# A decoder layer on one Trainium2 core: low parts of u finished in HBM by an adding DMA, and two more pairs by seven products

## The chip, the cores and the metric

The kernel runs on one core of one Trainium2 chip. The metric is the device time of one execution in microseconds. A core has five engines that each work through their own instructions in order: TensorE (PE, the matrix products), VectorE (DVE), ScalarE (ACT), GpSimd (POOL) and SyncE (SP). In this kernel SP and POOL mostly issue DMAs. Each engine waits on semaphores that the others, or landing DMAs, raise.

## The reference, cut to what matters

One decoder layer on 256 tokens of width 2048: a norm, an input projection, two attention groups, an output projection, and then the MLP, which is where the change lies:

```python
h = _rmsnorm(x, norm_mlp_pre[layer])
u = jnp.square(jax.nn.relu(h @ w_up[layer]))      # (256, 2048) @ (2048, 8192)
x = x + _rmsnorm(u @ w_down[layer], norm_mlp_post[layer])   # (256, 8192) @ (8192, 2048)
```

All arrays are float32.

## The kernel before

**Three products for one.** TensorE takes operands rounded to a shorter float format (`fp32r`). Each float32 operand `x` is therefore kept as a high part `hi`, which ACT makes by a rounding copy (line 306, or 310 with a gain), and a low part `lo = x - hi`, which DVE makes by a subtraction (line 307 or 311). A product then is three matmuls into one PSUM bank: hi·hi, hi·lo, lo·hi (`three`, line 1016).

**Weights.** `Weights` streams the weights of the whole program in one order. A tile is 128 rows by 1024 columns (512 KB); SP loads it into one of five buffers `raw`, ACT and DVE split it into one of eight pairs `hi`, `lo`. The load and the split of a tile are written at the same place of the program, six tiles ahead of the tile's use (`emit`, line 193). Because SP only issues loads, it runs further ahead than that, by as much as the five buffers allow.

**Pairs by seven products.** Two neighbouring weight tiles form a pair. Taken directly, a pair costs 2 tiles x 4 output banks x 3 = 24 matmuls of 512 columns. Taken by seven products (`seven_products`, line 1021; a Strassen-like scheme on 2x2 blocks) it costs 7 x 3 = 21, but needs sums of weights and of the left operand: three additions on DVE for the weights, four split tiles instead of two, and for the down projection `down_sums` and `down_split` for u. The two weight tiles of a pair are loaded by POOL as one DMA of 1 MB into `ab` and `ab2` (up projection) or `ab_down` and `c` (down projection).

**Up projection.** Eight blocks j = 0..7 of 1024 columns (line 1051). Blocks 2 to 6 each take tiles k8 to k11, then pair w0, k12, w1, k13, w2, k14, w3, k15. At the end of a block DVE adds the parts of the seven products to the four accumulators (lines 1043 and 1109), and the block's results are evacuated while the next block runs: `up_evac` (line 933) makes `r` = relu on ACT (line 937), has PE transpose it (`rt`, line 300), and ACT squares the transposed piece into `uT[g]` (line 949). Block j yields the two groups g = 2j and 2j+1 of u, 128 x 1024 each (4 k-tiles x 256 tokens), which stay in SBUF. `r` has two buffers.

**Down projection.** Two halves c = 0, 1 of 1024 output columns. Each runs over 64 k-tiles, four to a group g (`DOWN_STEPS`, line 120); `DOWN_SEVEN` (line 117) says which pairs go by seven products. `split_u` (line 951) prepares `uhi` and `ulo` of the next group, each with two buffers. In the first half ACT makes `uhi` and DVE makes `ulo`; `keep_u` (line 965) then has SP store `ulo` to HBM (`ukeep`), and in the second half POOL loads it back (line 960), so that DVE need not make it again. The split sums of pairs that are in both lists are kept in HBM in the same way (`SHARED`, `keep_s`, `down_back`).

**What sets the order.** The program is written in one thread of Python that follows the matmuls; `Flow` (line 128) holds a clock of estimated matmul time, and chains such as `up_evac` are generators that yield delays in microseconds. A chain's next piece is written into the engines' instruction streams when that clock has passed its time. Each engine then executes its stream strictly in that order.

Of the kernel before, what the change touches and what calls it, by code (L numbers as in the profile page):

```python
# [18 lines left out]
F32 = mybir.dt.float32  # L19
F32R = mybir.dt.float32r  # L20
I32 = mybir.dt.int32
BF16 = mybir.dt.bfloat16
AF = mybir.ActivationFunctionType
OP = mybir.AluOpType
PSUM = bass.MemoryType.PSUM

P = 128
# [18 lines left out]
CW = 1024  # L46
# [55 lines left out]
def up_steps(first, *groups):  # L102
    steps = [("k", k) for k in first]
    for i, ks in enumerate(groups):
# [9 lines left out]
N_SEVEN = [sum(w == "w" for w, _ in steps) for steps in UP_STEPS]  # L114


DOWN_SEVEN = ((7, 11, 13, 17, 19, 23, 25, 29), range(3, 28, 2))
SHARED = [k for k in DOWN_SEVEN[0] if k in DOWN_SEVEN[1]]
GT = FF // 512
DOWN_STEPS = [[s for kp in range(2 * GT)  # L120
               for s in ([("w", kp)] if kp in ws else [("k", 2 * kp), ("k", 2 * kp + 1)])] for ws in DOWN_SEVEN]

# [141 lines left out]
def layer(nc, tc, io):  # L264
    flow = Flow()
# [8 lines left out]
    dram = tc.alloc_tile_pool(name="dram", bufs=1, space=bass.MemoryType.DRAM)  # L274
# [3 lines left out]
    def bank(i, name):  # L278
        return ps.tile([P, 512], F32, tag=f"bank{i}", bufs=1, name=name)
# [19 lines left out]
    def transpose(out, a):  # L299
        nc.tensor.transpose(out, a, ident)  # L300
        flow.spend(TR)

    def split(hi, lo, src, g=None):
        if g is not None:
            return split_gain(hi, lo, src, g)
        nc.scalar.activation(hi, src, AF.Copy)  # L306
        nc.vector.tensor_tensor(out=lo, in0=src, in1=hi.bitcast(F32), op=OP.subtract)  # L307
# [6 lines left out]
    def tok(t, k, b):  # L314
        return t[:, k, b * P:(b + 1) * P]
# [28 lines left out]
    late = {}  # L344
# [85 lines left out]
    def seven_down(c, kp):  # L430
        def load():

            n = DOWN_SEVEN[c].index(kp)
            raw = dpl["ab"]
# [246 lines left out]
    for half in range(2):  # L681
        qkv = {}
        for nms in (("qk", "v") if not half else "qkv"):
            accs = [acc for _, _, acc in proj(xT, [ch_a[half, nms]], f"{nms}{half}",
                                              bank_of=at_bank if (half, nms) == (0, "v") else None)]
            for i, nm in enumerate(nms):
                t = pa.tile([P, NB, 512], F32, tag=nm, name=f"{nm}_{half}")
# [215 lines left out]
    for ns in ((0, 1), (2,), (3,)):  # L903
# [4 lines left out]
        for c, b, acc in proj(mixT, [ch_o[n] for n in ns], f"o{ns[0]}", order, heads_done):  # L908
            n = ns[c]
            if not late:  # L910
# [8 lines left out]
                                  in_=io["norm_attn_post"].partition_broadcast(P).rearrange("p o d -> p (o d)"))  # L919
# [8 lines left out]
    hT = late["hT"]  # L928


    uT = {}

    def up_evac(j, b, i, acc, order):

        yield UP_STEP * order
        r = late["up"].tile([P, 512], F32, tag="r", bufs=2, name=f"r{j}_{b}")
        nc.scalar.activation(r, acc, AF.Relu, scale=rstd2[b])
        yield D_UP if j > 1 else 2 * D_UP
        t = bank(i, f"rt{j}_{b}")
        for k in range(4):  # L940
            transpose(t[:, k * P:(k + 1) * P], r[:, k * P:(k + 1) * P])
        if j not in uT:
            if j in (0, 1, 10, 11, 12, 13):
                t2 = late["u01" if j < 2 else "ab2" if j < 12 else "ab"][:, j % 2 * CW:(j % 2 + 1) * CW]
            else:
                tag = {"tag": "T", "bufs": 2} if j > 13 else {}
                t2 = late["up"].tile([P, CW], F32, name=f"uT{j}", **tag)
            uT[j] = t2.rearrange("p (k s) -> p k s", k=4)
        nc.scalar.activation(uT[j][:, :, b * P:(b + 1) * P], t.rearrange("p (k s) -> p k s", k=4), AF.Square)

    def split_u(c, g):
        if (c, g) == (0, 0):
            uh, ul = [wp.tile([P, CW], F32R, tag=w, bufs=W_BUFS, name=f"u{w}0").rearrange("p (k s) -> p k s", k=4)
                      for w in ("hi", "lo")]
        else:
            uh, ul = [dpl["dp"].tile([P, 4, S], F32R, tag=f"u{w}", bufs=2, name=f"u{w}{c}_{g}") for w in ("hi", "lo")]
        u, h, l = [x.rearrange("p k s -> p (k s)") for x in (uT[g], uh, ul)]
        if c and g:
            nc.scalar.activation(h, u, AF.Copy)
            nc.gpsimd.dma_start(out=l.bitcast(F32), in_=ukeep[g])  # L960
        else:
            split(h, l, u)
        return uh, ul

    def keep_u(g):
        ukeep[g] = dram.tile([P, CW], F32, name=f"ukeep{g}")
        nc.sync.dma_start(out=ukeep[g], in_=us[0, g][1].rearrange("p k s -> p (k s)").bitcast(F32))

    def keep_s(kp):
        st, skeep[kp] = skeep[kp], dram.tile([P, CW], F32, name=f"skeep{kp}")  # L970
# [50 lines left out]
    def seven_products(ts, left, accs, m, first, last, m_first=False):  # L1021

        (a11, a12, a22), (s3, s1, s2, s4) = left
        prods = ((a11, 0, 0, 1), (a12, 1, 0, (0, 0)), (s4, 1, 1, (0, 1)), (s2, 2, 0, 6), (a22, 2, 1, (1, 0)),
                 (s3, 3, 1, 7), (s1, 3, 0, 5))
        if m_first:
            prods = sorted(prods, key=lambda x: not isinstance(x[3], int))
        for p, (a, i, half, to) in enumerate(prods):
            w = weights.get(ts[i])
            in_m = isinstance(to, int)  # L1030
            three(m[to] if in_m else accs[to], a, [w[x][:, half * 512:half * 512 + 512] for x in range(2)],
                  in_m and first, in_m and last)
            if all(x[1] != i for x in prods[p + 1:]):
                weights.free(ts[i])
            flow.pump()

    def close(c, m):

        tt = nc.vector.tensor_tensor
        nc.scalar.activation(c[0], m[1], AF.Copy)  # L1040
        for out, x, y, op in ((1, m[6], c[0], OP.subtract), (2, m[7], c[1], OP.subtract),
                              (3, m[5], c[2], OP.subtract), (1, m[5], c[1], OP.add)):
            tt(out=c[out], in0=x, in1=y, op=op)
        return dict(zip(PARTS, c))

    def closing():
        return [late["c"][:, i * 512:(i + 1) * 512] for i in range(4)]
# [3 lines left out]
    for j in range(FF // CW):  # L1051
# [9 lines left out]
        for t, b in order:  # L1061
            what, k, tiles = steps[t]
# [9 lines left out]
            if (j, t, b) == (FF // CW - 1, 4, 0):  # L1072
                weights.limit -= 1
                u_next = split_u(0, 0)
# [39 lines left out]
    up = late["up"]  # L1114
# [5 lines left out]
    def down_mm(c, u, k, b, n, w, first, last):  # L1120
        three(y[b][2 * c + n], [tok(u[x], k % 4, b) for x in range(2)], [t[:, 0, n * 512:n * 512 + 512] for t in w],
              first, last)

    def spare(i, n):

        return uT[i + n // 2].rearrange("p k s -> p (k s)")[:, (n % 2) * 512:(n % 2) * 512 + 512]
# [66 lines left out]
    late["st"] = up.tile([P, ST], F32, tag="st", bufs=1, name="st_down")  # L1193
    dpl["ab"] = dp.tile([P, 2 * CW], F32, name="ab_down")

    us, ukeep = {(0, 0): u_next}, {}
    for c in range(2):

        for i, (b, n) in enumerate(PARTS):
            y[b][2 * c + n] = bank(4 * c + i, f"y{b}{2 * c + n}")  # L1200
        accs = {(b, n): y[b][2 * c + n] for b, n in PARTS}
        ws = DOWN_SEVEN[c]
        for t, (what, k, tiles) in enumerate(wide_d[c]):
            g = (2 * k if what == "w" else k) // 4
            u = us[c, g]
            if g >= GT - 2 and c:
                break
            if what == "k":
                w = weights.get(tiles[0])
                for b, n in PARTS:  # L1210
                    down_mm(c, u, k, b, n, w, t == 0, t == len(wide_d[c]) - 1)
                    flow.pump()
                weights.free(tiles[0])
            else:
                if k == ws[0]:
                    if not c:
                        flow.finish(*u_last)
                    else:
                        flow.finish(h_evac)
                    m = {i: bank(4 * (1 - c) + o, f"md{i}_{c}") for o, i in enumerate((1, 6, 7, 5))}  # L1220
                blocks = [[tok(u[x], 2 * (k % 2) + kk, bb) for x in range(2)] for kk, bb in ((0, 0), (1, 0), (1, 1))]
                seven_products(tiles, (blocks, left.pop((c, k))), accs, m, k == ws[0], k == ws[-1])
                if k == ws[-1]:
                    more = close([spare(10, i) for i in range(4)] if c else closing(), m)
                if not c and k in SHARED:
                    keep_s(k)
            nxt = (c, g + 1) if g < GT - 1 else (1, 0)
            if nxt not in us:
                if not c and g > 1:
                    keep_u(g - 1)  # L1230
                us[nxt] = split_u(*nxt)
            if (c, what, k) == (0, "k", 3):
                weights.limit += 1
            if (c, what, k) == (0, "k", 36):
                g_half = [late["up"].tile([P, 512], F32, tag="r", bufs=2, name=f"g_half{n}") for n in range(2)]
                for n in range(2):
                    load_gain(n, g_half[n])
            if (c, what, k) == (1, "k", 40):
                flow.start(x_back())
                for n in (2, 3):  # L1240
                    load_gain(n, spare(4, n))
        if not c:
            keep_u(GT - 1)
            h_evac = flow.start(half_evac(more, g_half))

    tail = {k: tiles[0] for what, k, tiles in wide_d[1] if k >= 4 * (GT - 2) and what == "k"}
    for g in (GT - 2, GT - 1):
        for b, n in PARTS:
            for kk in range(4):
                k = 4 * g + kk  # L1250
# [58 lines left out]
```

## Time and profile before

| | |
|---|---|
| median of 3 runs | 1047.59 us (1047.38 to 1048.04) |
| profiled execution, its span | 1045.7 us |
| PE busy | 1035.7 us, 99% of the span |
| DVE busy | 838.7 us, 80% |
| ACT busy | 630.4 us, 60% |
| up projection, blocks 0 to 7 | about 354 to 701 us of the span |
| down projection, first half | about 702 to 861 us |
| down projection, second half | about 861 to 1039 us |

The span is that of one profiled execution, from its first to its last instruction; the median is of runs without the profiler and 1.9 us longer. A row of the time line gives start, duration, engine, line, operation, out<-in with shapes, and in brackets the idle time of the engine just before, with what ended it. "SPq" is SP's instruction queue.

### The profile page before, as it was taken

What the parts mean: (1) busy time and instruction counts of PE and PEld (TensorE: products, weight loads), DVE (VectorE), ACT (ScalarE), POOL (GpSimd) and SP (SyncE); (2) the same over time, 40 slices, a digit from 0 to 9 for tenths busy, and PEclk for the clock granted to TensorE, in tenths of its full rate; (3) what the DMA queues carried; (4) which work ended last, traced back from release to release, by engine and by line L of the source; (5) the groups of instructions that cost most, each with busy time, mean ns of one, the idle gap of its engine ahead of it and who ended that gap; (6) DMA issues with size and microseconds to landing.
All of it is one profiled execution on the core that took longest, in us unless ns stands there. A gap on an engine that the chain in (4) does not pass through costs nothing.

```text
span 1045.7 us, 13378 instructions
## 1 busy us (share of the span) xinstructions
PE 1035.7 (99%) x4837; PEld 863.2 (83%) x4837; DVE 838.7 (80%) x1122; ACT 630.4 (60%) x848; POOL 51.5 (5%) x83
## 2 busy tenths in 40 slices
PE   9999999999999999999999999999999999999996
PEld 6888889888888888888888888888888888888885
DVE  6676536567557669999999999897899978999995
ACT  6674436565545566665765667666567564766661
POOL 0000000000000000000000000000000000111100
PEclk9999999999999999999999999999999999999998
DMA  9975547454447295646657356378778767698952
GB/s 303 370 229 148 140 129 241 146 162 153 150 156 236 92 360 188 216 147 207 202 185 246 121 201 207 113 253 325 274 276 303 265 232 261 238 332 323 356 204 83
DMA packets 79938, 229.33 MB, mean 219 GB/s; under 512 B 6912, under 2 KB 11520, under 8 KB 79488
## 3 DMA queue, kind: packets, MB, share of 16 engines
q1 hardware_dynamic: 64576, 171.47, 48.9%
q0 software_dynamic: 14864, 56.63, 15.2%
q8 instruction: 38, 0.62, 0.3%
q10 hardware_dynamic: 432, 0.37, 0.1%
q14 instruction: 28, 0.23, 0.1%
HBM read 212.72 MB, written 15.73 MB: 218 GB/s over the span
## 4 chain that ended last, share of the span: by engine, by line
PE 97%; DVE 1%; issue 1%; ACT 0%; POOL 0%; DVEq 0%; POOLq 0%; ACTq 0%
PE y L296 25%; PE acc_u L296 24%; PE acc_o L296 8%; PE m L296 7%; PE md L296 5%; PE acc_qk L296 4%; PE acc_v L296 4%; PE acc_ckv L296 2%; PE acc_ukv L296 2%; PE acc_q L296 2%; PE acc_cq L296 2%; PE acc_k L296 2%; PE acc_uq L296 2%; PE rt L300 1%; PE sc_b L296 1%
## 5 line engine op out<-in xcount | busy, mean ns | idle before, releaser
L307 DVE TENSOR_TENSOR lo<-raw,hi 128x1024 fp32r<-128x1024 f32 (+3 forms) x213 | 241.5, 1152 | 89.8 <-ACT hi L306 89.1
L306 ACT ACTIVATE hi<-raw 128x1024 fp32r<-128x1024 f32 (+3 forms) x213 | 209.9, 999 | 73.6 <-PE y L296 16.1
L296 PE MATMUL y<-hi,uhi 128*128 128x512 f32 x370 | 144.4, 390 | 0.0
L296 PE MATMUL y<-hi,ulo 128*128 128x512 f32 x370 | 144.1, 389 | 0.0
L296 PE MATMUL y<-lo,uhi 128*128 128x512 f32 x370 | 144.0, 389 | 0.0
L296 PE MATMUL acc_u<-hi,hT_hi 128*128 128x512 f32 x356 | 141.7, 398 | 0.0
L296 PE MATMUL acc_u<-hi,hT_lo 128*128 128x512 f32 x356 | 139.2, 391 | 0.4 <-DVE hT_lo L307 0.4
L296 PE MATMUL acc_u<-lo,hT_hi 128*128 128x512 f32 x356 | 138.9, 390 | 0.0
L311 DVE SCALAR_TENSOR_TENSOR lo<-raw,gcol,hi 128x1024 fp32r<-128x1024 f32 x74 | 92.5, 1279 | 9.5 <-ACT hi L310 9.5
L310 ACT ACTIVATE hi<-raw,gcol 128x1024 fp32r<-128x1024 f32 x74 | 83.7, 1148 | 25.0 <-DMA raw<-in_w_up 11.7
L296 PEld LDWEIGHTS y<-hi,ulo 128*128 128x128 f32 x370 | 69.5, 188 | 14.4
L296 PEld LDWEIGHTS y<-lo,uhi 128*128 128x128 f32 x370 | 69.5, 188 | 14.3
L296 PEld LDWEIGHTS y<-hi,uhi 128*128 128x128 f32 x370 | 69.5, 188 | 14.2
L296 PEld LDWEIGHTS acc_u<-hi,hT_lo 128*128 128x128 f32 x356 | 66.8, 188 | 14.9 <-DVE hT_lo L307 0.8
L296 PEld LDWEIGHTS acc_u<-lo,hT_hi 128*128 128x128 f32 x356 | 67.0, 188 | 12.8
L296 PEld LDWEIGHTS acc_u<-hi,hT_hi 128*128 128x128 f32 x356 | 67.0, 188 | 12.8
L306 ACT ACTIVATE hi<-u 128x1024 fp32r<-128x1024 f32 (+1 forms) x38 | 37.4, 990 | 49.2 <-DVE u L366 35.4
L307 DVE TENSOR_TENSOR lo<-st_down,hi 128x1024 fp32r<-128x1024 f32 x42 | 50.4, 1220 | 3.0 <-ACT hi L306 2.8
L296 PE MATMUL acc_o<-hi,mixT_hi 128*128 128x512 f32 x128 | 51.8, 405 | 0.0
L306 ACT ACTIVATE hi<-st_down 128x1024 fp32r<-128x1024 f32 x42 | 43.9, 1052 | 12.6 <-PE y L296 9.5
L296 PE MATMUL acc_o<-hi,mixT_lo 128*128 128x512 f32 x128 | 50.2, 392 | 0.0
L296 PE MATMUL acc_o<-lo,mixT_hi 128*128 128x512 f32 x128 | 50.0, 391 | 0.0
(328 smaller groups left out, 2087.7 us busy)
## 6 DMA issues: line engine op xcount, KB each, us to landing
raw<-in_w_down SPq DMA_DIRECT2D x86, 512.0 KB, 5.8
raw<-in_w_up SPq DMA_DIRECT2D x76, 512.0 KB, 4.6
raw<-in_w_in SPq DMA_DIRECT2D x55, 512.0 KB, 4.9
ab<-in_w_up POOLq DMA_DIRECT2D x22, 1024.0 KB, 5.4
raw<-in_w_out SPq DMA_DIRECT2D x32, 512.0 KB, 4.2
ab_down<-in_w_down POOLq DMA_DIRECT2D x11, 1024.0 KB, 7.1
ukeep<-ulo SPq DMA_DIRECT2D x15, 512.0 KB, 7.0
ulo<-ukeep POOLq DMA_DIRECT2D x15, 512.0 KB, 6.2
```

The lines of the kernel that those rows point to most:

```text
L296: nc.tensor.matmul(out, a, b, start=start, stop=stop)
L300: nc.tensor.transpose(out, a, ident)
L306: nc.scalar.activation(hi, src, AF.Copy)
L307: nc.vector.tensor_tensor(out=lo, in0=src, in1=hi.bitcast(F32), op=OP.subtract)
L310: nc.scalar.activation(hi, src, AF.Copy, scale=g)
L311: nc.vector.scalar_tensor_tensor(out=lo, in0=src, scalar=g, in1=hi.bitcast(F32), op0=OP.mult, op1=OP.subtract)
```

## The change

The low part of u is no longer made by DVE in the first half of the down projection. For each group g from 1 to 15 a chain `lo_away(g)` starts when the group's second token block has been squared, 5 us (even g) or 12 us (odd g) later on the flow's clock. In two halves of 512 columns, ACT writes the negated high part into a tile `neg`, which takes one of the two buffers of `r`; 3 us later SP stores it to HBM (`ukeep[g]`); 9 us after that POOL issues a DMA that adds u itself to what lies there, which leaves u - hi. `split_u` then loads `ulo` from HBM in both halves for every group but g = 0. `keep_u` and its 15 stores are gone. `DOWN_SEVEN` gets ten pairs in the first half instead of eight, starting at pair 5 instead of 7; nine of them instead of seven are shared with the second half's list.

```diff
-DOWN_SEVEN = ((7, 11, 13, 17, 19, 23, 25, 29), range(3, 28, 2))
+DOWN_SEVEN = ((5, 7, 11, 13, 15, 19, 21, 23, 27, 29), range(3, 28, 2))
...
         nc.scalar.activation(uT[j][:, :, b * P:(b + 1) * P], t.rearrange("p (k s) -> p k s", k=4), AF.Square)
+        if b and j:
+            flow.start(lo_away(j), 5.0 + 7.0 * (j % 2))
+
+    def lo_away(g):
+
+        ukeep[g] = dram.tile([P, CW], F32, name=f"ukeep{g}")
+        u = uT[g].rearrange("p k s -> p (k s)")
+        for h in range(2):
+            c = slice(h * 512, (h + 1) * 512)
+            t = late["up"].tile([P, 512], F32, tag="r", bufs=2, name=f"neg{g}_{h}")
+            nc.scalar.activation(t.bitcast(F32R), u[:, c], AF.Copy, scale=-1.0)
+            yield 3.0
+            nc.sync.dma_start(out=ukeep[g][:, c], in_=t)
+            yield 9.0
+            nc.gpsimd.dma_start(out=ukeep[g][:, c], in_=u[:, c], accum_op=OP.add)
+            yield 2.0
...
-        if c and g:
+        if g:
             nc.scalar.activation(h, u, AF.Copy)
             nc.gpsimd.dma_start(out=l.bitcast(F32), in_=ukeep[g])
         else:
             split(h, l, u)
         return uh, ul
-
-    def keep_u(g):
-        ukeep[g] = dram.tile([P, CW], F32, name=f"ukeep{g}")
-        nc.sync.dma_start(out=ukeep[g], in_=us[0, g][1].rearrange("p k s -> p (k s)").bitcast(F32))
...
-                if not c and g > 1:
-                    keep_u(g - 1)
...
-            keep_u(GT - 1)
```

Three places of the instruction streams matter below, all at the turn from block 4 to block 5 of the up projection; the same order stands at the turns after blocks 2, 3 and 5. In the names, `raw230` is tile k15 of block 4, `raw231` to `raw234` are k8 to k11 of block 5, `raw239` is its k12, and the digits behind the underscore only count buffers.

SP, which issues the weight loads, before the change:

```order
L190 DMA raw225_4996<-in_w_up 128x1024
L190 DMA raw230_5051<-in_w_up 128x1024
L190 DMA raw231_5063<-in_w_up 128x1024
L190 DMA raw232_5084<-in_w_up 128x1024
L190 DMA raw233_5091<-in_w_up 128x1024
L190 DMA raw234_5100<-in_w_up 128x1024
L190 DMA raw239_5231<-in_w_up 128x1024
```

and now, with the stores of the negated parts (`neg6_1` is the second half of group 6):

```order
L190 DMA raw225_5045<-in_w_up 128x1024
L962 DMA ukeep7_5057<-neg7_0_5058 128x512
L190 DMA raw230_5105<-in_w_up 128x1024
L190 DMA raw231_5119<-in_w_up 128x1024
L962 DMA ukeep6_4974<-neg6_1_5114 128x512
L190 DMA raw232_5141<-in_w_up 128x1024
L190 DMA raw233_5148<-in_w_up 128x1024
L190 DMA raw234_5157<-in_w_up 128x1024
L962 DMA ukeep7_5057<-neg7_1_5191 128x512
L190 DMA raw239_5293<-in_w_up 128x1024
```

Four stores now stand among the eight loads of a block; the loads of k9, k10 and k11 stand behind the store of `neg6_1`.

ACT, which makes the high parts, at the same turn before the change:

```order
L310 ACTIVATE hi230_5053<-raw230_5051,gcol_69 128x1024
L310 ACTIVATE hi231_5065<-raw231_5063,gcol_69 128x1024
L310 ACTIVATE hi232_5086<-raw232_5084,gcol_69 128x1024
L310 ACTIVATE hi233_5093<-raw233_5091,gcol_69 128x1024
L310 ACTIVATE hi234_5102<-raw234_5100,gcol_69 128x1024
L1040 ACTIVATE c_3504<-m1_4_4894 128x512
L306 ACTIVATE hi235_5126<-ab_3502 128x512
L306 ACTIVATE hi236_5155<-ab_3502 128x1024
```

and now:

```order
L310 ACTIVATE hi230_5107<-raw230_5105,gcol_69 128x1024
L960 ACTIVATE neg6_1_5114<-uT6_4870 128x512
L310 ACTIVATE hi231_5121<-raw231_5119,gcol_69 128x1024
L310 ACTIVATE hi232_5143<-raw232_5141,gcol_69 128x1024
L310 ACTIVATE hi233_5150<-raw233_5148,gcol_69 128x1024
L310 ACTIVATE hi234_5159<-raw234_5157,gcol_69 128x1024
L1052 ACTIVATE c_3504<-m1_4_4939 128x512
L306 ACTIVATE hi235_5184<-ab_3502 128x512
L960 ACTIVATE neg7_1_5191<-uT7_4890 128x512
L306 ACTIVATE hi236_5215<-ab_3502 128x1024
```

`neg6_1` is written between the high parts of k15 and k8; the high part of k9 is the second instruction behind it.

POOL, which issues the loads of pairs, before the change:

```order
L374 DMA ab_3502<-in_w_up 128x2x1024
L374 DMA ab2_3503<-in_w_up 128x2x1024
L374 DMA ab_3502<-in_w_up 128x2x1024
L374 DMA ab2_3503<-in_w_up 128x2x1024
L374 DMA ab_3502<-in_w_up 128x2x1024
```

and now:

```order
L374 DMA ab2_3503<-in_w_up 128x2x1024
L964 DMA ukeep6_4974<-uT6_4870 128x512
L374 DMA ab_3502<-in_w_up 128x2x1024
L964 DMA ukeep7_5057<-uT7_4890 128x512
L964 DMA ukeep6_4974<-uT6_4870 128x512
L374 DMA ab2_3503<-in_w_up 128x2x1024
L964 DMA ukeep7_5057<-uT7_4890 128x512
```

Four adding DMAs stand among the four pair loads of a block; the load of pair w1 of block 5 (the last `ab2` shown) stands behind the adds of `neg7_0` and `neg6_1`, and each add waits until the store of its half has landed.

More of the change, by code (lines that the diff above doesn't have):

```diff
@@ L928, in layer @@
     hT = late["hT"]
-    uT = {}
+    uT, ukeep = {}, {}
     def up_evac(j, b, i, acc, order):
@@ L1194, in layer @@
     dpl["ab"] = dp.tile([P, 2 * CW], F32, name="ab_down")
-    us, ukeep = {(0, 0): u_next}, {}
+    us = {(0, 0): u_next}
     for c in range(2):
```

## The prediction

> **What bounds the kernel now.** I read the page first: span, busy shares, and the chain of work that ended last.
>
> ```profile
> span 1045.7 us, 13378 instructions
> PE 1035.7 (99%) x4837; PEld 863.2 (83%) x4837; DVE 838.7 (80%) x1122; ACT 630.4 (60%) x848; POOL 51.5 (5%) x83
> PE 97%; DVE 1%; issue 1%; ACT 0%; POOL 0%; DVEq 0%; POOLq 0%; ACTq 0%
> ```
>
> TensorE is the bound. Only fewer matmuls can shorten the time, and every wait of PE lengthens it. Next I cut the span into the blocks of the up projection and the first half of the down projection (length, then PE, weight loads, DVE, ACT, POOL busy, clock, DMA share, GB/s).
>
> ```profile
> 530.10:572.80 42.70, 42.70 (x198) 35.38 (x197) 41.01 (x46) 28.08 (x33) 2.85 (x4) 1.00 0.59 193
> 658.60:701.20 42.60, 42.60 (x197) 35.28 (x196) 37.63 (x43) 27.29 (x32) 0.00 (x0) 1.00 0.49 158
> 701.70:861.40 159.70, 159.70 (x714) 132.30 (x713) 136.88 (x153) 100.35 (x110) 6.42 (x9) 1.00 0.78 278
> ```
>
> PE has no idle time in any of them. But in block 4 DVE works 41.0 of 42.7 us: the up projection has a second engine that is almost as full, with 1.7 us to spare per block. In the first half of the down projection DVE has 22.8 us to spare.
>
> So I asked how near PE is to waiting in the up projection. The nearest place is the transposes of `r` just after a turn of blocks: PE's row, and ACT's rows ahead of it.
>
> ```profile
> 577.95 1.06 ACT L306 ACTIVATE hi<-u 128x1024 fp32r<-128x1024 f32 x1 [3.74 <-DVE u L366]
> 578.91 0.67 ACT L937 ACTIVATE r<-acc_u,rstd_pre 128x512 f32<-128x512 f32 x1
> ...
> 580.07 0.60 PE L300 MATMUL rt<-ident,r 128*128 128x128 f32 x4
> ```
>
> The second `r` of the turn ends at 579.58 and PE transposes it at 580.07: 0.5 us of room. That `r` stands on ACT behind `hi<-u`, which waits for DVE's sum `u`. DVE's rows say when that sum is made.
>
> ```profile
> 557.61 0.69 DVE L366 TENSOR_TENSOR u<-u,ab 128x512 f32<-128x512 f32 x1
> ...
> 563.43 6.06 DVE L311 SCALAR_TENSOR_TENSOR lo<-raw,gcol,hi 128x1024 fp32r<-128x1024 f32 x5
> 569.41 2.88 DVE L1043 TENSOR_TENSOR c<-m,c 128x512 f32<-128x512 f32 x4
> ...
> 572.80 2.49 DVE L1109 TENSOR_TENSOR acc_u<-acc_u,c 128x512 f32<-128x512 f32 x4
> ...
> 577.17 0.69 DVE L366 TENSOR_TENSOR u<-u,ab 128x512 f32<-128x512 f32 x1
> ...
> 581.05 1.23 DVE L307 TENSOR_TENSOR lo<-t,hi 128x1024 fp32r<-128x1024 f32 x1 [0.78 <-ACT hi L306]
> 582.19 1.22 DVE L361 TENSOR_TENSOR t<-ab 128x1024 f32<-128x1024 f32 x1
> ```
>
> From 557 to 580 DVE runs without a gap: five low parts (k15, then k8 to k11 of the next block, 1.2 us apart, the last one from 568.2), the closing sums, the additions, the next pair's sums. Whatever delays one of the five by more than 0.5 us delays `r`, and PE waits.
>
> **The change, part by part.**
>
> *Two pairs by seven products.* 48 matmuls become 42 for the two pairs. The chain of waits gives the pitch.
>
> ```profile
> 767.54 5.44 PE y L296 x24
> ...
> 934.17 5.44 PE y L296 x24
> 944.37 5.44 PE y L296 x24
> ```
>
> 5.44 / 24 = 0.227 us; six matmuls fewer are -1.36 us, all on the path. That is the whole gain to be had. The additions and splits that the pairs need, and the 15 low parts of u that DVE no longer makes, both lie under PE's full 159.7 us: they are costed at nothing, and freeing DVE there earns nothing. If that cover were gone, the added work of a pair would cost some 6 us of DVE time (the 2.6 us of its sums and 3 us of splits at the durations above), and each removed low part would give back 1.2 us.
>
> *ACT's negated copies.* Four per block. The nearest row is a rounding copy of the same shape:
>
> ```profile
> 553.99 0.63 ACT L306 ACTIVATE hi<-ab 128x512 fp32r<-128x512 f32 x1 [0.20 <-PE acc_u L296]
> ...
> 560.34 2.29 ACT L310 ACTIVATE hi<-raw,gcol 128x1024 fp32r<-128x1024 f32 x2
> 562.83 1.15 ACT L310 ACTIVATE hi<-raw,gcol 128x1024 fp32r<-128x1024 f32 x1 [0.21 <-PE m L296]
> 565.50 2.20 ACT L310 ACTIVATE hi<-raw,gcol 128x1024 fp32r<-128x1024 f32 x2 [1.52 <-PE acc_u L296]
> ```
>
> 4 x 0.63 = 2.5 us, under ACT's idle 14.6 us of a block; nothing by itself, at worst 2.5 us a block. `neg` takes buffers of `r`, but a store lands well before its buffer comes round again.
>
> *The stores on SP.* This is the expensive edit. SP issues in order, and before the change it did nothing but load, far ahead:
>
> ```profile
> SPq L190 <- DVE lo L311: 39.4, 8, 16.2
> 543.38 0.33 SPq L190 DMA_DIRECT2D raw<-in_w_up  x1
> DMA to landing us min/median/max: 3.4/4.2/6.5
> ```
>
> SP waits only for free buffers; the load of k9 went out at 543.38, 19 us ahead of its high part at 562.83. Now k9, k10 and k11 are queued behind the store of `neg6_1`, and that store waits for ACT to make `neg6_1`, just behind the high part of k15. By the rows: that high part ends at 561.5 (half of the 2.29), `neg6_1` at 562.1. Nothing behind the store can be issued earlier. What a store costs the queue:
>
> ```profile
> L967 SPq DMA_DIRECT2D ukeep<-ulo x15: 320/424/1514, 710.4 to 860.5; - x15
> 750.73 0.32 SPq L967 DMA_DIRECT2D ukeep<-ulo  x1
> 751.14 1.21 SPq L190 DMA_DIRECT2D raw<-in_w_down  x2
> GB/s 447 417 417 387 387 313 238 328 447 402 268 238 179 313 432 343 328 357 358 357 417 372 417 343 372 402 358 387 343 432 343 268 149 30 15 15 0 0 0 0
> ```
>
> 0.42 us for the issue, so k9 is issued at 562.5 and, with the median 4.2 us, lands at 566.7. The last row is a burst of five loads before an earlier turn; at its 360 GB/s, 512 KB take 1.46 us, so k11 lands 2.9 us after k9, at 569.6. Its high part takes 1.15: 570.8, against 568.2 when DVE wanted it. DVE is 2.6 us late, the closing sums, the additions and the next sums move by as much, `r` uses up its 0.5 us, and PE waits **2.1 us**. Bounds: if the load takes 3.4 us and the next two keep ACT's pace, the three high parts end at 569.35, DVE is 1.1 late and PE waits 0.6; at 6.5 us it ends at 573.1, DVE is 4.9 late, PE waits 4.4. I take 2.1, by the median row. The 0.78 us for which DVE waits at 581 let it recover what PE did not lose, so the next turn pays in full.
>
> The same order stands at four turns (after blocks 2 to 5): 4 x 2.1 = 8.4. At the turns after blocks 6 and 7 loads stand behind such a store too, and the room is at the third `r`:
>
> ```profile
> 666.60 1.26 ACT L937 ACTIVATE r<-acc_u,rstd_pre 128x512 f32<-128x512 f32 x2
> ...
> 667.97 0.60 PE L300 MATMUL rt<-ident,r 128*128 128x128 f32 x4
> ```
>
> The first of the two ends at about 667.3, 0.7 us ahead of PE. With the same lateness, 1.9 each, 3.8 together (0.4 to 4.2 each). The other three stores of a block hold back loads that have a whole pair's time, about 7 us, between copy and use: nothing.
>
> *The adding DMAs on POOL.* No row shows an accumulating DMA. Nearest rows:
>
> ```profile
> L960 POOL DMA_DIRECT2D ulo<-ukeep x15: 528/541/773, 872.6 to 1014.7; - x15
> DMA to landing us min/median/max: 2.9/6.5/10.1
> ...
> ab<-in_w_up POOLq DMA_DIRECT2D x22, 1024.0 KB, 5.4
> ...
> 561.54 0.71 POOL L374 DMA_DIRECT2D ab<-in_w_up  x1 [7.08 <-DVE lo L307]
> ```
>
> The pair load issued at 561.54 now waits for the add of `neg6_1`, that is until the store of 562.1 has landed (2.9 to 6.5 us): it goes out at 565.5 to 569 and lands 5.4 us later, 571 to 575, while its first reader stands at 582.19. At least 7 us remain: nothing. For an add itself I take what half a megabyte takes, 6.5 us, or less, overlapped with the loads. Its lower bound is a plain 2.9; its upper bound, 10.1, is in the second rival. The Trainium skill (DMA: Bandwidth & Descriptors, section Anatomy of one DMA — SWDGE (gpsimd) path) fits a POOL DMA by 2.0 us plus bytes over 436 GB/s; an estimate from that page is 2.6 us for 256 KB, with no price for adding. For a 1 MB load it gives 4.4 where the row here has 5.4, so it is rather low, and by it the second rival would be out and the sum unchanged.
>
> *The loads of `ulo` in the first half.* The second half does the same with a group each 10.2 us (934.17 to 944.37), 0.54 us to issue and 6.5 to land, and PE waits for none: nothing.
>
> Sum: -1.36 + 8.4 + 3.8 = **+10.8 us** (bounds +1.8 and +24.6). Against the profiled 1045.7 us that is 1056.5; the median lies 1.9 us above the span, so **1058.4 us**.
>
> **The rivals.**
>
> *It does what it says.* If SP reached the store with `neg6_1` done and the three loads landed by 567, only -1.36 us would remain: 1046.2. It decides below a lateness of 0.5 us. For it: PE's other margins are several us, and ACT has idle time. Against: no load in the row landed in under 3.4 us.
>
> *The adds fill POOL's queue.* Per block POOL has four loads of 5.4 and four adds. If they run one after another, the queue is full once an add takes (42.7 - 21.6) / 4 = 5.3 us; above that DVE waits for `ab` 4 us per block for each us more. At 6 us that is 2.8 in each of six blocks, which covers the turns' stalls only partly: 2.1 + 2.8, about 29 - 1.4, 1075. Against it: two DMAs of a queue overlap in the burst above.
>
> *The first half starves.* `ulo` is held by two buffers, and adds of the last groups stand between its loads on POOL. A load later than 10.2 - 0.54 = 9.7 us after its buffer is free makes PE wait; the row's longest landing is 10.1. If a third of 15 groups lost 1.5 us beside the turns: 1066.
>
> *Faster than the matmuls saved.* PE has no idle time that a lighter DVE could remove; nothing in the rows supports it.
>
> **How the numbers follow.** Differences under 0.2%, 2.1 us, can't be told from no change here. Late loads at the turns: 0.62, 1058.4, own range 1049.4 to 1072. It does what it says: 0.17 (no difference). Full POOL queue: 0.10. First half: 0.08. Faster: 0.03. Slower is 0.80, the same 0.17, faster 0.03. The range leaves out the rival at 1046.2 and the far end of the first one: 1048.5 to 1070.
>
> **What would show it.** Right: in the new profile ACT idles at each turn's second or third `hi<-raw` with the DMA as releaser, about 4 us; SP waits for ACT at line 962; DVE idles some 2.6 us there; PE idles at line 300 behind `r`; blocks 2 to 5 take about 44.8 us instead of 42.7, and the first half of the down projection 1.4 us less than 159.7. Wrong: blocks of 42.7 us; ACT waiting for nothing at the turns; or DVE waiting at line 361 for `ab`, which would put the loss on POOL; or PE gaps after 702, on `ulo`.

## The result and the profile after

The changed kernel takes 1091.45 us (median of 4 runs, 1088.46 to 1094.8) beside 1047.68 us (1047.38 to 1048.04) for the kernel before: ratio 1.0418, 95% interval 1.0401 to 1.0436. It is slower by 43.8 us, where +10.8 us was predicted. The profiled execution has a span of 1093.0 us. From its page, the same parts as were shown of before:

```profile
span 1093.0 us, 13493 instructions
PE 1049.9 (96%) x4831; PEld 865.7 (79%) x4831; DVE 831.7 (76%) x1117; ACT 644.4 (59%) x882; POOL 89.0 (8%) x132
PE 70%; DMA 12%; DVE 10%; issue 4%; ACT 4%; SPq 0%; POOL 0%; DVEq 0%; ACTq 0%; POOLq 0%
```

PE is still busy for 96% of the span, but the chain of waits, which was 97% PE, now runs through DMAs for 12% and through DVE for 10%. Of the 47.3 us by which the span is longer, PE is idle for 33.1 more. It executes 6 matmuls fewer and is nevertheless busy 14.2 us longer; the section on why the prediction was wrong comes back to that. Two blocks of the up projection, from one block's additions (line 1121, the former 1109) to the next one's, with the columns of the earlier table (length, PE, weight loads, DVE, ACT, POOL, clock, DMA share, GB/s):

```profile
494.29:542.34 48.05, 44.55 (x199) 35.36 (x198) 41.33 (x45) 29.73 (x37) 6.24 (x9) 0.99 0.71 218
542.34:591.18 48.84, 44.78 (x198) 35.96 (x197) 41.35 (x45) 29.72 (x37) 6.40 (x8) 0.97 0.69 211
```

A block of 42.7 us has become one of 48 to 49, with the same DVE work in it (41.3 us) but no longer back to back. The first `y` matmul starts at 737.46 instead of 701.56 us: 35.9 of the lost microseconds lie in the up projection, 11.5 behind it. From the list of waits of the stretch 420 to 760 us (engine, line, releaser: sum, times, longest):

```profile
POOL ukeep L964 <- DMA ukeep<-neg: 199.8, 23, 17.5
...
ACT hi L310 <- DMA raw<-in_w_up: 47.1, 19, 7.3
...
DVE lo L311 <- ACT hi L310: 30.3, 14, 6.1
...
PE acc_u L296 <- ACT c L1052: 11.6, 5, 3.7
PE rt L300 <- ACT r L937: 10.3, 6, 2.8
```

The second row and those below it form a chain: the weight loads come too late for ACT, the high parts therefore too late for DVE, and PE waits at two places, not one. The first row is POOL's wait for the stores, which by itself costs PE nothing. The turn from block 4 to block 5 on the time line shows the order of events:

```profile
569.50 0.69 DVE L366 TENSOR_TENSOR u<-u,ab 128x512 f32<-128x512 f32 x1
...
575.65 1.16 ACT L310 ACTIVATE hi<-raw,gcol 128x1024 fp32r<-128x1024 f32 x1 [3.34 <-DMA raw<-in_w_up]
576.72 0.61 ACT L960 ACTIVATE neg<-uT 128x512 fp32r<-128x512 f32 x1
...
577.36 0.33 SPq L962 DMA_DIRECT2D ukeep<-neg  x1
577.77 1.37 SPq L190 DMA_DIRECT2D raw<-in_w_up  x3
...
580.02 0.88 POOL L964 DMA_DIRECT2D ukeep<-uT  x1 [4.95 <-DMA ukeep<-neg]
580.59 1.05 POOL L374 DMA_DIRECT2D ab<-in_w_up  x1
582.85 3.71 ACT L310 ACTIVATE hi<-raw,gcol 128x1024 fp32r<-128x1024 f32 x3 [4.47 <-PE acc_u L296]
584.03 3.85 DVE L311 SCALAR_TENSOR_TENSOR lo<-raw,gcol,hi 128x1024 fp32r<-128x1024 f32 x3 [4.34 <-ACT hi L310]
586.47 0.58 ACT L1052 ACTIVATE c<-m 128x512 f32<-128x512 f32 x1
587.10 0.79 PE L296 MATMUL acc_u<-hi,hT_hi 128*128 128x512 f32 x1 [2.28 <-ACT c L1052]
...
598.02 0.66 PE L300 MATMUL rt<-ident,r 128*128 128x128 f32 x4 [1.73 <-ACT r L937]
```

k15 keeps ACT waiting until 575.65, so `neg6_1` is written at 576.72, its store leaves at 577.36, and the three loads behind it (k9, k10, k11) leave together from 577.77. In the same three microseconds POOL, released by the same store, issues an adding DMA and the next pair load. ACT idles 4.47 us before the high part of k9 (the view names a PE event as the releaser, but PE had long been done; the load landed just then), and `c<-m` comes at 586.47. The next block's accumulators use the banks that hold `m`, so PE waits there 2.28 us, and 11 us later 1.73 us at the transposes of the second `r`. How long the loads took to land (the three that leave at 577.8, then the one of k15, which left behind the store of `neg7_0`):

```profile
L190 SPq DMA_DIRECT2D raw<-in_w_up x3: 371/383/416, 577.8 to 578.8; - x3
DMA to landing us min/median/max: 5.0/5.8/6.5
...
L190 SPq DMA_DIRECT2D raw<-in_w_up x1: 388/388/388, 567.8 to 567.8; - x1
DMA to landing us min/median/max: 7.8/7.8/7.8
```

One number measures the whole delay: from the end of the third pair's sum `u` (570.19) to the start of the last of the five low parts. The x3 row ends at 587.88, its last subtraction takes 1.28, so that start is 586.60 and the stretch 16.4 us; before, it was 568.2 - 558.3 = 9.9. DVE is 6.5 us late where the prediction had 2.6. Over the four turns the stretch is 16.2, 15.6, 16.4 and 16.3 us, a mean lateness of 6.2, and the blocks grow by 6.3, 5.4, 6.1 and 6.0.

### The profile page after: what moved, and what is told of

Same layout as the page of the kernel before. It is cut to its first block, busy times and chain, and to the rows that moved or that the text cites. A ratio compares the mean times of both kernels' runs of the same rounds, so it can differ in the third digit from the quotient of the medians.

```text
span 1093.0 us, 13493 instructions
## 1 busy us (share of the span) xinstructions
PE 1049.9 (96%) x4831; PEld 865.7 (79%) x4831; DVE 831.7 (76%) x1117; ACT 644.4 (59%) x882; POOL 89.0 (8%) x132
## 4 chain that ended last, share of the span: by engine, by line
PE 70%; DMA 12%; DVE 10%; issue 4%; ACT 4%; SPq 0%; POOL 0%; DVEq 0%; ACTq 0%; POOLq 0%
PE y L296 20%; PE acc_u L296 10%; PE acc_o L296 8%; DMA raw<-in_w_up 6%; PE md L296 5%; PE acc_qk L296 4%; PE acc_v L296 4%; DVE lo L307 3%; PE acc_ckv L296 2%; DMA raw<-in_w_down 2%; PE acc_q L296 2%; PE acc_ukv L296 2%; PE acc_cq L296 2%; PE acc_k L296 2%; DVE lo L311 2%
## 5 line engine op out<-in xcount | busy, mean ns | idle before, releaser
L307 DVE TENSOR_TENSOR lo<-raw,hi 128x1024 fp32r<-128x1024 f32 (+3 forms) x209 | 236.7, 1150 | 100.4 <-ACT hi L306 99.6
L306 ACT ACTIVATE hi<-raw 128x1024 fp32r<-128x1024 f32 (+3 forms) x209 | 205.6, 997 | 91.7 <-DMA raw<-in_w_down 25.4
L296 PE MATMUL acc_u<-hi,hT_hi 128*128 128x512 f32 x356 | 145.6, 409 | 13.9 <-ACT c L1052 11.6
L296 PE MATMUL y<-hi,uhi 128*128 128x512 f32 x358 | 142.0, 397 | 4.0 <-ACT c L1052 4.0
L296 PE MATMUL y<-lo,uhi 128*128 128x512 f32 x358 | 141.1, 394 | 2.5 <-DVE lo L307 2.5
L296 PE MATMUL y<-hi,ulo 128*128 128x512 f32 x358 | 141.1, 394 | 1.5 <-DMA ulo<-ukeep 1.5
L296 PEld LDWEIGHTS y<-hi,ulo 128*128 128x128 f32 x358 | 68.3, 191 | 16.3 <-DMA ulo<-ukeep 1.9
L296 PEld LDWEIGHTS acc_u<-hi,hT_lo 128*128 128x128 f32 x356 | 67.7, 190 | 15.6 <-DVE hT_lo L307 0.8
L306 ACT ACTIVATE hi<-u 128x1024 fp32r<-128x1024 f32 (+1 forms) x38 | 37.2, 987 | 41.3 <-DVE u L366 31.5
L307 DVE TENSOR_TENSOR lo<-st_down,hi 128x1024 fp32r<-128x1024 f32 x46 | 55.2, 1221 | 1.1 <-ACT hi L306 1.0
L306 ACT ACTIVATE hi<-st_down 128x1024 fp32r<-128x1024 f32 x46 | 47.8, 1050 | 4.0 <-DVE st_down L366 3.2
```

The lines of the kernel that those rows point to most:

```text
L296: nc.tensor.matmul(out, a, b, start=start, stop=stop)
```

## The experiments

Each median is of 4 to 11 runs and stands beside runs of the kernel before on the same chip (1047.6 to 1047.8 us). "First y" is the start of the first `y` matmul in the profiled execution, "rest" what follows it.

| kernel | median us | ratio, 95% interval | first y | rest |
|---|---|---|---|---|
| before | 1047.6 | | 701.6 | 344.1 |
| the change | 1091.5 | 1.0418, 1.0401 to 1.0436 | 737.5 | 355.6 |
| ten pairs only | 1047.8 | 0.9999, 0.9990 to 1.0007 | 703.0 | 343.8 |
| low parts in HBM only | 1083.9 | 1.0349, 1.0335 to 1.0363 | 733.7 | 348.5 |
| stores on ACT's queue | 1055.7 | 1.0071, 1.0056 to 1.0086 | 702.4 | 350.3 |
| no adds | 1080.9 | 1.0314, 1.0298 to 1.0330 | 726.6 | 353.1 |
| first halves' stores on ACT | 1090.1 | 1.0403, 1.0385 to 1.0420 | 731.8 | 358.2 |
| second halves' stores on ACT | 1065.2 | 1.0173, 1.0156 to 1.0190 | 710.5 | 350.3 |
| stores on ACT, groups 1 to 11 | 1047.7 | 1.0002, 0.9993 to 1.0011 | 703.0 | 344.1 |
| the same, 13 pairs | 1054.6 | 1.0064, 1.0049 to 1.0079 | 701.7 | 349.5 |
| before with stores of 16 columns on SP | 1072.2 | 1.0234, 1.0220 to 1.0248 | 722.5 | 348.8 |
| before, ten pairs without pair 21 | 1047.0 | 0.9993, 0.9984 to 1.0003 | 701.8 | 343.6 |
| before, 11 pairs | 1051.9 | 1.0043, 1.0030 to 1.0055 | 702.7 | 347.7 |
| stores on ACT, groups 1 to 11, 11 pairs | 1046.5 | 0.9989, 0.9980 to 0.9998 | 701.4 | 342.1 |

### One half of the change each

Ten pairs in the kernel before:

```diff
-DOWN_SEVEN = ((7, 11, 13, 17, 19, 23, 25, 29), range(3, 28, 2))
+DOWN_SEVEN = ((5, 7, 11, 13, 15, 19, 21, 23, 27, 29), range(3, 28, 2))
```

> Only the list of pairs is changed (ten instead of eight in the first half); the low parts of u are made by DVE and stored by SP as before. If the loss comes from the new chain for the low parts, this runs without it: six matmuls fewer, -1.4 us, 1046.3. If the two more pairs load DVE or start too early (pair 5 instead of 7), PE waits at the start of the down projection: 1050 or more.

Measured 1047.8: no gain that could be told. And the converse, the change with the old eight pairs:

```diff
-DOWN_SEVEN = ((5, 7, 11, 13, 15, 19, 21, 23, 27, 29), range(3, 28, 2))
+DOWN_SEVEN = ((7, 11, 13, 17, 19, 23, 25, 29), range(3, 28, 2))
```

> Only the new chain (negated copies, stores, adding DMAs, loads of ulo in both halves), with the old list of eight pairs. If the chain carries the loss: 1092 to 1094, the changed kernel's time plus about 1.4 us. If the pairs carry it: about 1048.

Measured 1083.9. The low parts made in HBM carry 36 of the 43.8 us by themselves. The pairs, free when alone, cost 7.5 more on top of them; in the profiled executions most of that lies behind the first `y` (355.6 us there against 348.5).

### Where the stores are issued

```diff
-            nc.sync.dma_start(out=ukeep[g][:, c], in_=t)
+            nc.scalar.dma_start(out=ukeep[g][:, c], in_=t)
```

> The changed kernel, with the stores of the negated parts issued by ACT instead of SP; the same bytes move and POOL waits for the same stores. Theory 1 (stores that wait for ACT hold back the weight loads queued behind them on SP): blocks 2 to 5 of the up projection go back from 48.7 to 43-44 us, in all 1048 to 1056. Rival A (the adding DMAs and their traffic delay the loads): blocks stay at 47 us or more, above 1080.

Measured 1055.7. One block of it, then what is left behind 702 us (ACT, PE, POOL and DVE on the time line, and the store issued at 704.0):

```profile
530.73:573.42 42.69, 42.69 (x198) 35.35 (x197) 41.00 (x45) 29.69 (x37) 6.50 (x8) 1.00 0.83 249
```

```profile
711.19 0.69 ACT L937 ACTIVATE r<-acc_u,rstd_pre 128x512 f32<-128x512 f32 x1 [1.63 <-DMA ukeep<-neg]
...
711.93 0.33 PE L300 MATMUL rt<-ident,r 128*128 128x128 f32 x1 [2.09 <-ACT r L937]
...
758.54 0.88 POOL L964 DMA_DIRECT2D ukeep<-uT  x1 [8.55 <-DMA ukeep<-neg]
759.11 1.04 POOL L374 DMA_DIRECT2D c<-in_w_down  x1
...
769.46 1.23 DVE L361 TENSOR_TENSOR st_down<-c 128x1024 f32<-128x1024 f32 x1 [7.96 <-DMA c<-in_w_down]
...
773.33 0.50 PE L296 MATMUL y<-lo,uhi 128*128 128x512 f32 x1 [1.51 <-DVE lo L307]
```

```profile
L962 ACTq DMA_DIRECT2D ukeep<-neg x1: 326/326/326, 704.0 to 704.0; - x1
DMA to landing us min/median/max: 7.2/7.2/7.2
```

The same copies, the same bytes, the same adds, more traffic per microsecond (DMA share 0.83): and the block is back at 42.69 us with PE full. It was the place of the stores in SP's queue that stretched the blocks. Of the 8.0 us that remain, most lie in the down projection (6.2 of 7.0 in the profiled execution). `r` waits for a store, because `neg` takes one of its two buffers and the store took 7.2 us to land. A pair load leaves late behind an add that itself waited 8.55 us for its store; DVE waits 7.96 us for that pair, and PE then waits 1.51 us for a low part that stands on DVE behind the pair's sums.

### The adds

```diff
-            nc.gpsimd.dma_start(out=ukeep[g][:, c], in_=u[:, c], accum_op=OP.add)
```

Without the adds `ulo` is only the negated high part.

> The changed kernel without the adding DMAs (it leaves out u + (-hi): what is loaded as ulo is -hi); the stores stay on SP. Theory 1: the turns still wait for the loads behind the stores, but those land with less traffic beside them: blocks of 45 to 47 us, 1065 to 1080. Rival A: blocks of 43 us, 1046 to 1050.

Measured 1080.9, so leaving out the adds gives 10.5 us back; they are not the main cause. A block:

```profile
540.17:587.65 47.48, 43.90 (x198) 34.89 (x197) 41.14 (x46) 29.73 (x37) 2.86 (x4) 1.00 0.56 196
```

The blocks are still 47 to 49 us long. That is theory 1, and the time is just above its 1065 to 1080. With all the adds but the stores on ACT's queue blocks 2 to 5 are within 0.1 us of the kernel before, so there the adds cost nothing unless the stores stand on SP. For the size of an add, the changed kernel between 420 and 760 us (the row of 16 of the 26 adds there; the landing is of all 26):

```profile
L964 POOL DMA_DIRECT2D ukeep<-uT x16: 861/880/924, 467.9 to 641.7; - x16
...
DMA to landing us min/median/max: 3.8/4.9/9.4
```

256 KB with an add take 4.9 us to land (median), 0.88 us to issue. The longest landing of all 30 is 16.2 us.

### Which stores

```diff
-            nc.sync.dma_start(out=ukeep[g][:, c], in_=t)
+            (nc.sync if h else nc.scalar).dma_start(out=ukeep[g][:, c], in_=t)
```

> The stores of the first halves (neg*_0) go out on ACT's queue, those of the second halves (neg*_1) stay on SP, where the loads of k9, k10 and k11 stand behind neg*_1. Stores all on SP gave 1091.5, all on ACT 1055.7. Theory 1, the prediction's place alone: DVE is 2.6 us late at a turn, PE waits about 2.1 us at the transposes of the second r, blocks 2 to 5 take about 44.8 us, 1055.7 + about 10 = 1066. Theory 2, the load of k15 behind neg*_0 carries most of the loss: with it gone the blocks take under 43.3 us and the time is 1056 to 1059. Theory 3, each place alone is as dear as both: blocks of 48 us, 1085 or more.

and the converse, `(nc.scalar if h else nc.sync)`:

> The converse: the stores of the second halves (neg*_1) go out on ACT's queue, those of the first halves (neg*_0) stay on SP, where the load of k15 stands behind neg7_0 at a turn. Theory 1 (the place of neg*_1 alone counts): blocks of 42.8 us, 1056. Theory 2 (k15 carries most): ACT waits about 3 us for k15, c<-m and the second r come later, blocks of 46 to 48 us, 1075 to 1085. If the two add up, this one and its converse together account for 1091.5 - 1055.7 = 35.8 us; if they need each other, both stay near 1056 to 1060.

Measured 1090.1 and 1065.2. A block of each, and how the three loads behind `neg6_1` landed in the first:

```profile
541.10:589.24 48.14, 44.36 (x197) 35.56 (x196) 41.19 (x46) 29.67 (x37) 6.51 (x9) 0.98 0.71 215
...
L190 SPq DMA_DIRECT2D raw<-in_w_up x3: 382/385/398, 573.1 to 574.0; - x3
DMA to landing us min/median/max: 4.6/7.2/9.3
```

```profile
535.49:580.43 44.94, 43.22 (x198) 35.15 (x197) 41.18 (x45) 29.63 (x37) 6.50 (x8) 1.00 0.75 233
```

The predicted place, the second halves' stores ahead of k9 to k11, gives nearly the whole loss by itself (42.5 of 43.8 us), so theory 3 of the first expectation holds for it. Only its size is far from the 2.1 us per turn of theory 1. The first halves' stores ahead of k15 are not free either: the block shown is 2.2 us longer, and the stretch on DVE is 12.5 us instead of 9.9. The two don't add up, 34.4 + 9.5 against 35.8 above the version with all stores on ACT; the section on why the prediction was wrong says why.

### The wait without the bytes

The kernel before, plus the copies, plus stores of 16 columns instead of 512 to a scratch tensor, issued on SP at the change's places:

```diff
+        if b and j:
+            flow.start(lo_away(j), 5.0 + 7.0 * (j % 2))
...
+            nc.scalar.activation(t.bitcast(F32R), u[:, c], AF.Copy, scale=-1.0)
+            yield 3.0
+            nc.sync.dma_start(out=scratch[:, h * 16:(h + 1) * 16], in_=t[:, :16])
+            yield 9.0
+            yield 2.0
```

> The kernel before, with ACT's negated copies and SP's stores at their new places, but each store carries 16 of the 512 columns into a scratch tensor that nothing reads; no adds, low parts of u by DVE as before. The wait of SP's queue is whole, the bytes are gone. Theory 1 (the wait alone, with loads that land as the prediction reckoned: k9 4.2 us after its issue, k11 7.1): DVE 2.6 us late at a turn, 2.1 us of PE for each, 1047.6 + 12 = 1060. Theory 2 (three loads that leave together, beside a pair load, land later than that, and every turn pays at two places, at the accumulators' banks and at the second r): blocks of 46 to 48 us, 1070 to 1081, near the version without adds (1080.9). Theory 3 (the bytes of the stores, not the wait): under 1052.

Measured 1072.2. A block, the landing of the loads of k9 to k11 at the turn into block 5, and their high parts on ACT:

```profile
539.24:585.29 46.05, 43.60 (x198) 34.96 (x197) 41.15 (x46) 29.74 (x37) 2.86 (x4) 1.00 0.51 179
...
L190 SPq DMA_DIRECT2D raw<-in_w_up x3: 382/391/498, 571.2 to 572.2; - x3
DMA to landing us min/median/max: 5.7/6.5/7.2
...
576.97 3.70 ACT L310 ACTIVATE hi<-raw,gcol 128x1024 fp32r<-128x1024 f32 x3 [5.16 <-PE m L296]
```

That is theory 2. The wait alone costs 24.5 us, more than half of the loss and twice the predicted 12.2 for the turns, with hardly a byte in the stores and the DMA engines half idle (share 0.51). The bytes of the stores are not the main cause. At this turn the stretch on DVE is 13.6 us: 3.7 late instead of 2.6. The high part of k9 starts at 576.97; its load left at 571.2 and took 5.7 us to land, not 4.2, beside a pair load that POOL had issued at 570.30.

### What is left, and the pairs

Stores on ACT's queue, and only groups 1 to 11 made in HBM; groups 12 to 15, whose stores and adds fall into the turn to the down projection, by DVE and `keep_u` as before:

```diff
-        if b and j:
+        if b and 0 < j < 12:
...
-        if g:
+        if g and (c or g < 12):
```

> Stores on ACT's queue, and only groups 1 to 11 made in HBM; groups 12 to 15 by DVE in the first half and stored by SP, as before. Theory 1 (what is left of the loss, 1055.7 - 1047.7, comes from the stores and adds of the last groups: r waits at 711 for the store whose tile shares its two buffers, and the pair load at 759 stands behind an add): both waits of PE, 2.1 and 1.5 us, and the half clock at 712.8 are gone; 1047 to 1049. Rival (the second half, or ulo's loads in general, costs it): 1053 or more.

Measured 1047.7: the 8.0 us are gone, and with them the whole loss. With 13 pairs on top:

> The same with 13 pairs by seven products in the first half (5, 7, ... 29) in place of ten. If DVE's relief pays for pairs, 18 matmuls fewer at 0.227 us are worth 4.1 us less than the version with ten, 1044 by theory 1. Rival (DVE, POOL's pair loads or the sums' loads of the second half become late): each additional pair costs DVE about 6 us of some 10 spare, PE waits in the first half, and the time is 1048 or more.

Measured 1054.6, the rival: PE waits for low parts of u in the last quarter of the first half, and once 2.04 us in the second half for a low part that stands on DVE behind a pair's sums.

Why do two more pairs earn nothing? In the kernel before with ten pairs PE waits once in the second half:

```profile
965.10 0.55 POOL L404 DMA_DIRECT2D s<-skeep  x1 [8.43 <-PE md L296]
965.64 0.53 POOL L960 DMA_DIRECT2D ulo<-ukeep  x1
...
976.03 0.50 PE L296 MATMUL y<-hi,ulo 128*128 128x512 f32 x1 [0.58 <-DMA ulo<-ukeep]
```

Pair 21 is now among the shared ones. Its kept sum is read back just ahead of `ulo`, amid a stretch of other loads. So, with pair 17 in its place, in the kernel before:

```diff
-DOWN_SEVEN = ((7, 11, 13, 17, 19, 23, 25, 29), range(3, 28, 2))
+DOWN_SEVEN = ((5, 7, 11, 13, 15, 17, 19, 23, 27, 29), range(3, 28, 2))
```

> The kernel before with ten pairs by seven products in the first half, but pair 17 in place of pair 21 of the new list. With pair 21 the second half reads a kept sum back at 965.10 us, ahead of the low part of u issued at 965.64, which lands after 10.35 us, and PE waits 0.58 us for it. Theory 1 (that late load ate the gain of the two pairs): with 21 out, no such wait, and 6 matmuls less at 0.227 us are seen: 1046.2, ratio 0.9987. Rival (the gain is lost elsewhere, in the clock or at the end): 1047.6, ratio 1.000.

Measured 1047.0, ratio 0.9993 with an interval that holds both the forecast and 1. The wait at 976 is gone, but PE now waits 0.40 us at 798.58 for a low part of u on DVE. That is inconclusive as a time; the trace shows the one wait exchanged for another. Pair 9 added, without and with the low parts of u in HBM (stores on ACT, groups 1 to 11):

> The same with 11 pairs, 9 added. If nothing becomes late, 9 matmuls fewer than before: 1047.6 - 2.0 = 1045.6, ratio 0.998. DVE gets about 5.3 us more work than with ten pairs, 153 of 157.7 us of the first half: if that is too near, PE waits for low parts in the first half and the time is 1047 or more.

> Stores on ACT's queue, groups 1 to 11 made in HBM, and the 11 pairs without pair 21. DVE has 13 us less to do in the first half than the version with the low parts on it. Theory 1 (late load of the second half gone): 1045.6, and the difference to the 11 pairs alone shows what the low parts made in HBM earn; rival (the adds or stores still cost something at a turn, as the 0.96 us wait at 666.79 of the version with ten pairs): 1047.

Measured 1051.9 and 1046.5. The first half of the former, what its weight loads on PE waited for there, and both halves of the latter:

```profile
702.80:863.00 160.20, 156.81 (x692) 127.91 (x691) 150.69 (x177) 99.89 (x115) 8.56 (x12) 1.00 0.82 278
...
PEld y L296 <- DVE ulo L307: 3.7, 4, 0.9
```

```profile
701.40:859.70 158.30, 158.30 (x708) 131.08 (x707) 141.85 (x169) 103.37 (x119) 14.48 (x23) 1.00 0.83 289
859.70:1035.20 175.50, 175.50 (x775) 145.06 (x773) 153.91 (x176) 104.19 (x121) 22.32 (x38) 1.00 0.77 271
```

With DVE at 150.7 of 160.2 us PE waits for the low parts of u. With eleven of them taken off DVE, PE is full in both halves, and the time lies between the two forecasts. What is left of the change in this form is a gain of 0.11% (0.02% to 0.20%). It is the only version here whose whole interval lies below 1, and by so little that the prediction's own measure, 0.2%, would not tell it from no change.

## Why the prediction was wrong

**Right: the bound, the sign and the place.** The load path behind a store on SP decides. Stores off SP bring the blocks back to 42.69 us; the second halves' stores alone bring nearly all of the loss. ACT idles ahead of the high part of k9, as forecast, for 3.5 to 4.5 us at the first three turns and 7.1 us at the fourth.

**Right: how lateness turns into PE time.** "Whatever delays one of the five by more than 0.5 us delays `r`" held within a few tenths. A lateness of 2.6 us (12.5 - 9.9, the second halves' stores on ACT) lengthened that block by 2.2 us, 3.7 (the small stores) by 3.4, 6.2 on average (the change) by 6.0. That PE pays part of it at the accumulators' banks, behind `c<-m`, was not seen; it moves the place, not much of the sum.

**Wrong, the main step: the lateness itself, 2.6 us.** It measured 6.2, beyond the upper bound of 4.9. The forecast had put it together from an issue of k9 at 562.5, 4.2 us after the third pair's sum (558.3), and from landings that bring k11 in 7.1 us after that issue. At the first three turns of the changed kernel the landings came out as reckoned: k11 landed 6.6 to 7.5 us after the issue of k9. The issue was late: 577.77 - 570.19 = 7.6 us after the sum at the turn shown, 7.6 to 8.0 at the three, because `neg6_1` stood on ACT behind a high part of k15 that was late itself. What failed there is the next step below, a term put at nothing. At the fourth turn k15 was nearly in time and k9 left 4.8 us after the sum, but the landings were too long:

```profile
623.88 1.98 SPq L190 DMA_DIRECT2D raw<-in_w_up  x3
...
DMA to landing us min/median/max: 7.6/8.4/8.6
```

There k11 landed 10.1 us after the issue of k9, so the term "with the median 4.2 us" was mis-sized: that row is of loads which mostly go out one by one, far ahead, and here three leave together, near a pair load and an add. The same shows when k15 is not held back at all. With only the second halves' stores on SP, k9 left 4.1 us after the sum at all four turns, as forecast, and k11 landed 8.9 to 12.1 us after it. So either fault alone makes a turn 4.4 to 7.6 us late. That is why removing the first halves' stores from SP gave back only 1.3 us, and why the two halves don't add up. The turns after blocks 6 and 7 were mis-sized too: PE waits there 3.66 + 1.09 and 3.98 + 2.82 us, where 1.9 each were reckoned.

**Wrong: "the other three stores of a block hold back loads that have a whole pair's time", "nothing".** The load of k15 stands behind the store of `neg7_0`. Before the change ACT took up k15 2.0 us after the third pair's sum, which here would be 572.2. The load left at 567.8, so it had 4.4 us, not 7; it landed 7.8 us after its issue and ACT waited 3.34 us for it (3.3 to 3.8 at the first three turns). Everything behind it on ACT, `neg6_1` first, moved by as much. With only these stores on SP the time is still 9.5 us above the version with none there.

**Wrong: "the adding DMAs on POOL", "nothing".** With the stores on SP they cost 10.5 us. Each waits on POOL for its store and moves 256 KB beside SP's loads. In the profile without them the load of k15 took 5.5 to 6.7 us at the first three turns instead of 7.8 to 8.0, but blocks 2 to 5 are together only 2.6 us shorter; block 6 and the stretch behind it to the first `y` are 7.9 us shorter. The rival that they fill POOL's queue falls as the main cause: without them 33.3 us of the loss remain. By the Trainium skill (DMA: Bandwidth & Descriptors, section Anatomy of one DMA — SWDGE (gpsimd) path) the estimate for one was 2.6 us, and that page does not price the add. The measured median is 4.9.

**Wrong: "a store lands well before its buffer comes round again".** With the stores on ACT's queue, one at the turn to the down projection took 7.2 us and `r` waited for its buffer. This wait, the half clock behind it and the late pair load are most of the 8.0 us that remain in that version.

**Wrong: "-1.36 us, all on the path".** In the kernel before, ten pairs gave 1047.8. In the profiled execution the matmuls from the first `y` to the last take 0.51 us less than before, not 1.36; a wait of 0.58 us in the second half is most of the difference. Three further waits, 1.1 us together, stand in the first 13 us of the program, and whether they belong to the edit one profile can't say. "Freeing DVE there earns nothing" holds for the old list; for 11 pairs it decides, 1046.5 against 1051.9.

**Not in the sum at all: the clock.** The granted clock of the changed kernel is 0.989 on average, of before 0.997. Two of the six stretches behind a wait of PE:

```profile
586.93:590.33 3.40, 3.23 (x7) 2.32 (x8) 3.19 (x5) 2.10 (x4) 0.00 (x0) 0.50 0.45 170
...
812.21:815.61 3.40, 3.40 (x10) 2.63 (x9) 3.33 (x7) 0.00 (x0) 0.00 (x0) 0.50 0.89 320
```

Seven or eight matmuls start in such a stretch, where 15 fit at 0.227 us each, so PE loses about 1.7 us in it. Six of them are about 10 us by this estimate, which is most of PE's 14.2 us of additional busy time; in the kernel before there is none but at the very end.

What stays open: the 8.8 us between the version with small stores (1072.2) and the one without adds (1080.9) come from the stores' bytes, the pairs and the loads of `ulo` together, and were not taken apart. Nor was it taken apart how much of the long landings comes from the three loads being together and how much from the pair load and the add beside them.

## What to carry to other kernels

A store that waits for a compute engine makes a prefetching DMA queue as late as that engine: before putting one there, list the loads behind it, and reckon that they will all come out at once, together with whatever else the store releases. Do this for every store, also the ones that seem to have time: here a load held back by one store made the engine late that had to feed the next store. The Trainium skill (DMA: Bandwidth & Descriptors, section Issuing engines are not separate DMA queues) says that spreading DMAs over engines saves only the time of initiating them. Here another issuing engine for 30 stores saved 35.8 us, because a queue also passes on its waits. For such a burst, take a landing time from rows in which as many transfers leave together, not the median of loads that leave one by one.

## What the runs showed of the hardware

A wait of PE of 2 us or more mostly cost about 1.7 us or more beyond its length. In fourteen profiled executions, of the 21 waits of PE of 2.04 us or more behind the start of the program, 19 were followed or overlapped by a stretch of 3.4 or 6.8 us with the clock at 0.5; the other two were of 2.15 and 2.77 us. Of the 40 waits from 0.9 to 1.93 us, two were. The Trainium skill (TensorE: Matmul & The Clock Gate, section HAM oscillation — how this bites in real kernels) gives "no PE-idle gaps >~3.4µs" as its rule. Here waits of 2.04 us, six tenths of that, were enough, while the 3.4 us for which the clock stays low agree with the window of that length of which the page speaks.

An adding DMA is dear on the DMA engines, too. POOL's queue in the version without adds and in the changed kernel (packets, MB, share of the 16 engines' span):

```profile
q0 software_dynamic: 17856, 67.64, 17.8%
...
q0 software_dynamic: 22176, 75.50, 21.5%
```

Without adds that is 192.2 of 1079.7 us for 67.64 MB, 2.8 us per MB, the same as in the kernel before (15.2% of 1045.7 us for 56.63 MB). The 7.86 MB of adds (30 of 256 KB) raise it to 235.0 of 1093.0 us: 42.8 us, 5.4 per MB, nearly twice as much. The figure includes whatever the adds do to the other transfers of that queue.
